# Loading the parameters first, four more warm-up matmuls, and the gate exponentials moved behind the last convolution tile

## The chip, the cores and the metric

The kernel runs on one core of one Trainium2 chip. The metric is the device time of one execution in microseconds (us). TensorE is called PE in the profile (its weight loads PEld), VectorE DVE, ScalarE ACT, GpSimd POOL, and SyncE, which here only issues DMAs, SP.

## What is computed

One decoder layer for a prompt of 512 tokens and a sample group of 8 x 8 tokens, 576 columns in all, model width 1024. The part that matters here is the first third:

```
u    = rms(x) * g_pre_mix;   proj = u @ w_in          # 1024 x 5656
z, xbc, dt_raw, q, k, v, ig, fg, og = split(proj)
xbc  = silu(causal_conv(xbc))                         # 12 tiles of 128 channels
dt   = softplus(dt_raw + dt_bias);  a = -exp(a_log)   # the gates
h'   = h * exp(cum[-1]) + sum_s exp(cum[-1]-cum_s) dt_s x_s B_s     # SSD state, per chunk
y    = (C B^T * exp(cum_t - cum_s) * dt) x + (C h) * exp(cum_t)
mLSTM heads from q, k, v, ig, fg with the same kind of chunk decays; then w_out
...                                                   # cross-attention, SwiGLU
```

## The kernel before, in words

Activations lie transposed: 128 features on the partitions, 576 tokens in the free dimension, eight such blocks `k`. A float32 product is made of three matmuls in a reduced float32 format: high part times high part, high times low, low times high. So each weight tile `raw` is split into `whi` (a cast, ACT, L186) and `wlo` (the rest, DVE L193, or ACT L190 and an accumulating DMA from POOL, L191), and the activations into `uh` and `ul`. The matmuls of a tile go in two halves of the tokens, 256 and 320 wide.

**The start.** PE first runs `NWARM` matmuls on a zeroed tile `wz` (L309, written to `ps_warm`, which nobody reads). Meanwhile SP and ACT issue the loads: for the first two weight tiles 256 columns at a time (`raws[0]`, `raws[1]`), the eight blocks of x (`xraw`), and `par`, a table of 128 x 150 numbers with all gains and biases. ACT makes `uh` from `xraw` and the gain in `par` (L333), DVE makes `ul` (L334). Then PE runs the first two weight tiles block by block (L350 to L352), the third (`w2`, L208 to L211), the sums of squares of x by a product with ones (`ps_ss`, L234), and the fourth tile (`w3`). ACT and DVE in the meantime split `w2`, sum the squares of x into `ssqx` (L270 to L275), and split `w3`.

**Convolution and gates.** `conv_tile(j, dst)` makes one of 12 convolution tiles: PE product, DVE eviction into `cb`, ACT and DVE taps into `ac`, and two Silu activations on ACT, 512 and 64 wide (L498, L500). Ahead of j = 4 the gate tile and the first q tile are put in. A chain of small operations on ACT and DVE turns the gates into running sums, which PE transposes (`ps_ct`) and spreads (`ps_en`). Seven exponentials on ACT, 4 to 64 columns wide, follow (L601 to L612): `decp` and `wend` (SSD decay and weight of each token in its chunk's end state), `scalem` and `wendm` (the same for mLSTM), `expnm`.

**The SSD part.** `ssd_prompt` takes four chunks in turn: PE transposes x (`ps_xt`), DVE scales it (`xdt`), POOL multiplies by `wend` (`xe`, L650), PE multiplies by B's tokens `btok` (`ps_h`, L652), POOL and DVE carry the state on (`hs`). PE mixes these with the products of q, k and v tiles (`ps_in`, `ps_v`), which need nothing of the gates.

Silu and Exp lie in different activation tables. The build step puts an ACT_TABLE_LOAD in front of an activation whose table is not the loaded one. The order of each engine's instructions in this part is set by a scheduler when the kernel is built; `tc.high_priority(offset=1000)` around the block from `ps_ct` on pulls it forward, and `tc.issue_after(x)` keeps what stands under it behind the instruction x.

Of the kernel before, what the change touches and what calls it, by code (L numbers as in the profile page):

```python
# [14 lines left out]
AF = mybir.ActivationFunctionType  # L15
# [5 lines left out]
T = 576  # L21
TP = 512
TS = 64
# [83 lines left out]

CUT = 512
CCUT = 128
NWARM = 17  # L110
NSS = 7
NWX = 3
TCOPT = dict(schedule_with_timeline_sim=True)
# [2 lines left out]
def build(nc, tc, ctx, I, O):  # L116
    V, A, G, S, TE = nc.vector, nc.scalar, nc.gpsimd, nc.sync, nc.tensor
# [21 lines left out]
    def MP(name="m"):  # L139
        return pa.tile([P, 512], F32, name=name, tag="a")  # L140
# [12 lines left out]
    par = cp.tile([P, NPAR], F32, name="par")  # L153

    def C32(k):
        a, b = _c32[k]
        return c32[:, a:b] if b <= NLONG else c32e[:, a - NLONG:b - NLONG]
# [5 lines left out]
    def PAR(k, j=None, w=1):  # L163
        a, b = _cols[k]
        return par[:, a:b] if j is None else par[:, a + j:a + j + w]
# [30 lines left out]
    def split(hi, lo, src, eng=None, cast=None):  # L196
        c = (cast or A.copy)(hi, src)  # L197
        (eng or V).tensor_tensor(lo, src, hi.bitcast(F32), op=ALU.subtract)  # L198
        return c
# [93 lines left out]
    wendm = ml.tile([P, 5, 4], F32, name="wendm")  # L293
    scalem = ml.tile([P, 4, 4], F32, name="scalem")
# [12 lines left out]
    psw = MP("ps_warm")  # L307
    for _ in range(NWARM):
        mm(psw[:, 0:256], wz[:, 0:128], wz, start=True, stop=True, skip_group_check=True)  # L309

    wl = [wp.tile([P, 1024], F32R, name="wlo", tag="wlo", bufs=3) for _ in range(2)]
    RT = {k: wp.tile([P, 3], F32, name=k + "_r", tag=k + "_r") for k in ("px0", "p30", "px1", "p31")}
# [2 lines left out]
    for k in range(KT):  # L315
        if k % 2 == 0:
            c = slice(128 * k, 128 * k + 256)
            S.dma_start(raws[0][:, c], I["win"][1][:, c])
        if k == 0:
            S.dma_start(par, I["par"])  # L320
        xd = (S if k else A).dma_start(xraw[:, k, :], I["xT"][:, k, :])
        if k % 2 == 0:
            xd = (S if k else A).dma_start(raws[1][:, c], I["win"][2][:, c])
        if k == 0:
            with tc.issue_after(xd.ins), tc.high_priority(offset=300):

                A.activation(sp.tile([P, 1], F32, name="one"), wz[:, 0:1], AF.Exp)

        if k == 0:
            V.tensor_copy(wi[0][0][:, c], raws[0][:, c])  # L330
        for t0, n in ([(0, T)] if k else HALVES):
            ts_ = slice(t0, t0 + n)
            uhk = A.activation(uh[:, k, ts_], xraw[:, k, ts_], AF.Copy, scale=PAR("g_pre", k))  # L333
            ulk = V.scalar_tensor_tensor(ul[:, k, ts_], xraw[:, k, ts_], PAR("g_pre", k), uh[:, k, ts_].bitcast(F32),  # L334
                                         op0=ALU.mult, op1=ALU.subtract)
        if k % 2 == 0:
            for i in range(2):
                with tc.issue_after(uhk.ins), tc.issue_after(ulk.ins):
                    split(wi[i][0][:, c], wi[i][1][:, c], raws[i][:, c], cast=None if k or i else lambda *_: None)
# [54 lines left out]
    def in_tile(i, evac, cut=CUT):  # L394

        if i < 5:
            for (t0, n), ps in zip(HALVES, ps0[i - 1]):
                if i == 4 and t0:
                    with tc.issue_after(rows[-1].ins):
                        gemm(ps, [(*w3, KT)], U, UL, t0, n, 2, KT)  # L400
                evac(t0, n, xs[:, 5 + i, t0:t0 + n] if i < 3 else ps)
        else:
            if i not in fetched:
                fetch(i, cut)
            w = fetched.pop(i)
            if i in behind:
                gemm2([(*w, KT)], U, UL, evac, "ps_in", [0])
            with tc.issue_after(behind[i].ins) if i in behind else ExitStack():
                gemm2([(*w, KT)], U, UL, evac, "ps_in", [1] if i in behind else [0, 1])
# [11 lines left out]
    wend = bcp.tile([P, 5, 16], F32, name="wend")  # L421
    decp = bcp.tile([P, 4, 16], F32, name="decp")
# [35 lines left out]
    cst = cv.tile([P, 12, NB, 3], F32, name="cst")  # L458
    S.dma_start(cst, I["convst"])

    late_rows, last_in = [], [5]

    def conv_tile(j, dst):

        cb = cv.tile([P, 604], F32, name="cb", tag="cb", bufs=2)
        sm = cb[:, CS:CB].rearrange("p (b t) -> p b t", t=11)

        def ev(t0, n, ps):
            V.tensor_tensor(cb[:, 3 + t0:259 + t0], ps[:, 0:256], rxb[:, t0:t0 + 256], op=ALU.mult)
            if t0:  # L470
                V.tensor_tensor(sm[:, :, 3:11], ps[:, 256:320].rearrange("p (b t) -> p b t", t=8),
                                rxb[:, TP:T].rearrange("p (b t) -> p b t", t=8), op=ALU.mult)

        in_tile(1 + j, ev, CUT if j == 4 else 0)
        with ExitStack() as after:
            if 4 <= j < 10:
                for i in range(2 + j, 4 + j):
                    if i > last_in[0]:
                        fetch(i, 0)
                        last_in[0] = i  # L480
                after.enter_context(tc.issue_after(accs[-1].ins))
            if late_rows:
                late_rows.pop()()
            G.memset(cb[:, 0:3], 0.0)
            G.tensor_copy(sm[:, :, 0:3], cst[:, j, :, :])

        def rows_out():
            G.tensor_copy(convo[:, j, 0:3], cb[:, CS - 3:CS])
            G.tensor_copy(convo[:, j, 3:27].rearrange("p (b t) -> p b t", t=3), sm[:, :, 8:11])

        late_rows.append(rows_out)
        e = V
        ac = cv.tile([P, 604], F32, name="ac", tag="ac", bufs=2)
        A.activation(ac[:, 0:600], cb[:, 0:600], AF.Identity, scale=PAR("convw", 4 * j), bias=PAR("convb", j))
        for k in range(1, 4):
            e.scalar_tensor_tensor(ac[:, 0:600], cb[:, k:600 + k], PAR("convw", 4 * j + k), ac[:, 0:600],
                                   op0=ALU.mult, op1=ALU.add)
        A.activation(dst[:, 0:TP], ac[:, 0:TP], AF.Silu)  # L498
        sa = ac[:, CS:CB].rearrange("p (b t) -> p b t", t=11)
        A.activation(dst[:, TP:T].rearrange("p (b t) -> p b t", t=8), sa[:, :, 0:8], AF.Silu)  # L500


    qk = SL(1, "qk")
# [82 lines left out]
    with tc.high_priority(offset=1000):  # L586
        psc = MP("ps_ct")
        for c in range(4):
            TE.transpose(psc[:, c * 104:c * 104 + 100], r1[:, c * P:(c + 1) * P], ident[0:100, 0:100])
            TE.transpose(psc[:, c * 104 + 100:c * 104 + 104], r2[:, c * P:(c + 1) * P], ident[0:4, 0:4])  # L590
        A.copy(CT[:, 0:4, :], psc[:, 0:416].rearrange("p (c k) -> p c k", c=4))
        psc = MP("ps_ct2")
        TE.transpose(psc[:TS, 0:100], r1[:, TP:T], ident[0:100, 0:100])
        TE.transpose(psc[:TS, 100:104], r2[:, TP:T], ident[0:4, 0:4])
        A.copy(CT[:TS, 4, :], psc[:TS, 0:104])
        pse = MP("ps_en")
        mm(pse[:, 0:416], C32("e127"), CT[:, 0:4, :].rearrange("p c k -> p (c k)"), start=True, stop=True)
        en = pse[:, 0:416].rearrange("p (c k) -> p c k", c=4)
        V.tensor_tensor(wend[:, 0:4, :], en[:, :, 0:16], CT[:, 0:4, 0:16], op=ALU.subtract)
        V.tensor_tensor(wendm[:, 0:4, :], en[:, :, 96:100], CT[:, 0:4, 64:68], op=ALU.add)  # L600
        A.activation(decp, en[:, :, 0:16], AF.Exp)  # L601
        A.activation(scalem, en[:, :, 96:100], AF.Exp)
        pse = MP("ps_en2")
        mm(pse[:TS, 0:104], C32("esamp")[:TS, :], CT[:TS, 4, :], start=True, stop=True)
        V.tensor_tensor(wend[:TS, 4, :], pse[:TS, 0:16], CT[:TS, 4, 0:16], op=ALU.subtract)
        V.tensor_tensor(wendm[:TS, 4, :], pse[:TS, 96:100], CT[:TS, 4, 64:68], op=ALU.add)
        A.activation(wend[:, 0:4, :], wend[:, 0:4, :], AF.Exp)
        A.activation(wendm[:, 0:4, :], wendm[:, 0:4, :], AF.Exp)
        A.activation(wend[:TS, 4, :], wend[:TS, 4, :], AF.Exp)
        wd = A.activation(wendm[:TS, 4, :], wendm[:TS, 4, :], AF.Exp)  # L610
        with tc.issue_after(wd.ins):
            A.activation(expnm, CT[:, 0:4, 100:104], AF.Exp, scale=-1.0)  # L612
        V.tensor_scalar(ncum, CT[:, 0:4, 0:16], -1.0, None, op0=ALU.mult)
# [126 lines left out]
    for g in range(2):  # L740
        for hb in range(2):
            dst = cpad[:, g, 4 * hb:4 * hb + 4, :].rearrange("p b t -> p (b t)")
# [5 lines left out]
    for g in range(2):  # L748
# [13 lines left out]
        for h in range(8):  # L762
            k, j = h % 2, (8 * g + h) // 2
# [164 lines left out]
    for h in range(4):  # L928
        q, k = qk[:, h, :], qk[:, 4 + h, :]
# [1488 lines left out]
```

## Time and profile before

| | |
|---|---|
| runs | 1078.0, 1080.8, 1081.1 us, median 1080.8 |
| profiled execution | 1079.13 us, its span 1077.4 us |
| busy share of the span | PE 99%, PEld 94%, DVE 70%, ACT 56%, POOL 21% |
| chain that ended last | PE 93%, DVE 3%, ACT 1%, DMA 1% |
| HBM | 159.75 MB read, 20.65 MB written |

The busy time of PE is modelled and includes the way through the array, so whether PE moves at its full pace is better read from the distance between the starts of two matmuls. In a row of the timeline the first number is the start, the second the duration, and the bracket holds the idle time in front with what ended it.

### The profile page before, as it was taken

The page shows a single profiled execution, that of the slowest core. Times are in us where ns is not written, and L with a number is a line of the kernel's source. Part 1 is how long each engine was busy: PE and PEld are TensorE (multiplying, and loading weights), DVE is VectorE, ACT ScalarE, POOL GpSimd, SP SyncE. Part 2 cuts the span into 40 slices and gives each one's busy share as a digit, 9 for nine tenths or more (in the row PEclk, how much of TensorE's full clock was granted, in tenths as well). Part 3 has the DMA queues.
Part 4 walks back from the last instruction along what each step waited for, and adds up shares of the span by engine and source line. Part 5 has one row for each costly group of instructions (what it writes and reads, how often), then busy time and mean ns, then how long its engine had stood idle before and what let it go on. Part 6 is the DMA issues. An engine that isn't in the chain of part 4 may idle for free.

```text
span 1077.4 us, 20699 instructions
## 1 busy us (share of the span) xinstructions
PE 1067.5 (99%) x8120; PEld 1015.1 (94%) x8120; DVE 752.0 (70%) x1509; ACT 607.8 (56%) x1094; POOL 231.5 (21%) x305
## 2 busy tenths in 40 slices
PE   9999999999999999999999999999999999999997
PEld 8999887778999999999999889999999999999997
DVE  6798775658877775559755555766467887787556
ACT  7778532345654555656555445645566566656653
POOL 0453643313213111000154301100011111111000
PEclk9999999999999999999999999999999999999998
DMA  6787544426655449743468775644476697588532
GB/s 208 164 171 133 159 127 177 147 73 183 191 153 145 111 120 329 254 169 109 147 206 286 268 257 176 241 131 93 136 181 140 155 201 167 116 190 184 130 132 89
DMA packets 58822, 181.76 MB, mean 169 GB/s; under 512 B 6588, under 2 KB 11836, under 8 KB 58212
## 3 DMA queue, kind: packets, MB, share of 16 engines
q1 hardware_dynamic: 42740, 138.06, 39.1%
q0 software_dynamic: 15408, 41.43, 20.0%
q8 instruction: 64, 1.05, 0.4%
q10 hardware_dynamic: 576, 0.95, 0.3%
q14 instruction: 34, 0.28, 0.1%
HBM read 159.75 MB, written 20.65 MB: 167 GB/s over the span
## 4 chain that ended last, share of the span: by engine, by line
PE 93%; DVE 3%; ACT 1%; DMA 1%; issue 1%; POOL 0%; DVEq 0%; SPq 0%; ACTq 0%
PE ps_in L208 6%; PE ps_in L211 6%; PE ps_in L209 6%; PE ps_v L854 5%; PE ps_o L211 3%; PE ps_g L1910 3%; PE ps_g L1909 3%; PE ps_o L209 3%; PE ps_g L1911 3%; PE ps_o L208 3%; PE ps_u L1910 3%; PE ps_u L1911 3%; PE ps_u L1909 3%; PE ps_dn L1909 2%; PE ps_dn L1910 2%; PE ps_dn L1911 2%
## 5 line engine op out<-in xcount | busy, mean ns | idle before, releaser
L211 PE MATMUL ps_in<-uh,wlo 128*128 128x320 f32 (+1 forms) x544 | 161.6, 298 | 0.0
L208 PE MATMUL ps_in<-uh,whi 128*128 128x320 f32 (+1 forms) x544 | 161.6, 297 | 0.0
L209 PE MATMUL ps_in<-ul,whi 128*128 128x320 f32 (+1 forms) x544 | 160.9, 296 | 0.0
L186 ACT CAST whi<-raw 128x1024 fp32r<-128x1024 f32 (+1 forms) x104 | 105.4, 1014 | 96.3 <-PE ps_in L209 30.2
L193 DVE TENSOR_TENSOR wlo<-raw,whi 128x1024 fp32r<-128x1024 f32 (+2 forms) x97 | 94.8, 979 | 61.8 <-ACT whi L186 57.3
L211 PEld LDWEIGHTS ps_in<-uh,wlo 128*128 128x128 f32 x544 | 102.2, 188 | 2.0 <-issue 1.3
L208 PEld LDWEIGHTS ps_in<-uh,whi 128*128 128x128 f32 x544 | 102.3, 188 | 1.5 <-issue 0.8
L209 PEld LDWEIGHTS ps_in<-ul,whi 128*128 128x128 f32 x544 | 102.3, 188 | 0.4
L191 POOL DMA_DIRECT2D wlo<-win x31 | 27.2, 876 | 76.0 <-ACT wlo L190 64.7
L1909 PE MATMUL ps_g<-b,whi 128*128 128x288 f32 x144 | 42.4, 295 | 0.0
L1910 PE MATMUL ps_g<-b,whi 128*128 128x288 f32 x144 | 42.4, 295 | 0.0
L1910 PE MATMUL ps_u<-b,whi 128*128 128x288 f32 x144 | 42.2, 294 | 0.0
L1909 PE MATMUL ps_u<-b,whi 128*128 128x288 f32 x144 | 42.2, 294 | 0.0
L1882 ACT CAST whi<-rawx 128x1024 fp32r<-128x1024 f32 (+1 forms) x26 | 25.7, 987 | 27.7 <-PE ps_dn L1910 13.7
L198 DVE TENSOR_TENSOR wlo<-sw,whi 128x1024 fp32r<-128x1024 f32 (+1 forms) x26 | 29.6, 1140 | 15.5 <-ACT whi L197 15.4
L208 PE MATMUL ps_xo<-qh,whi 128*128 128x288 f32 x128 | 38.4, 302 | 0.1
L211 PE MATMUL ps_o<-mixm_h,wlo 128*128 128x256 f32 (+1 forms) x128 | 37.7, 295 | 0.0
L209 PE MATMUL ps_xo<-ql,whi 128*128 128x288 f32 x128 | 37.7, 296 | 0.0
L209 PE MATMUL ps_o<-mixm_l,whi 128*128 128x256 f32 (+1 forms) x128 | 37.5, 293 | 0.0
L211 PE MATMUL ps_xq<-u2h,wlo 128*128 128x320 f32 (+1 forms) x128 | 37.5, 294 | 0.0
L209 PE MATMUL ps_xq<-u2l,whi 128*128 128x320 f32 (+1 forms) x128 | 37.4, 294 | 0.0
L211 PE MATMUL ps_o<-mixs_h,wlo 128*128 128x320 f32 (+1 forms) x128 | 37.4, 292 | 0.0
(770 smaller groups left out, 3848.6 us busy)
## 6 DMA issues: line engine op xcount, KB each, us to landing
raw<-win SPq DMA_DIRECT2D x35, 512.0 KB, 4.1
raw<-wout SPq DMA_DIRECT2D x17, 512.0 KB, 4.0
raw<-wxq SPq DMA_DIRECT2D x13, 512.0 KB, 4.0
raw<-wgate SPq DMA_DIRECT2D x13, 512.0 KB, 3.6
raw<-wup SPq DMA_DIRECT2D x13, 512.0 KB, 5.0
wlo<-win POOLq DMA_DIRECT2D x24, 256.0 KB, 5.1
kva<-vc SPq DMA_DIRECT2D x11, 512.0 KB, 6.5
raw<-wv SPq DMA_DIRECT2D x10, 512.0 KB, 4.1
```

Of the source, the lines that this page charges most:

```text
L186: casts.append(A.copy(hi[:, :n], raw[:, :n]))
L191: accs.append(G.dma_start(lo[:, a:b], src[:, a:b], accum_op=ALU.add))
L193: e.tensor_tensor(lo[:, a:b], raw[:, a:b], hi[:, a:b].bitcast(F32), op=ALU.subtract)
L198: (eng or V).tensor_tensor(lo, src, hi.bitcast(F32), op=ALU.subtract)
L208: mm(ps, wh, ah, start=i == 0, stop=False)
L209: mm(ps, wh, al, start=False, stop=False)
L211: m = mm(ps, tiles[order[c]][1], xh(order[c], t0, n), start=False, stop=c == len(tiles) - 1)
L854: mm(ps, a, b, skip_group_check=True, **kw)
L1882: A.copy(s.h3[:, s.all], s.r2[:, s.all])
L1909: mm(ps, wh, b[0][k], start=start and k == 0, stop=False, skip_group_check=True)
L1910: mm(ps, wh, b[1][k], start=False, stop=False, skip_group_check=True)
L1911: m = mm(ps, wl, b[0][k], start=False, stop=k == nk - 1, skip_group_check=True)
```

## The change

`NWARM` goes from 17 to 21. The load of `par` is issued right behind the warm-up matmuls in program order, ahead of the first piece of weights, and no longer between weights and x. The second Silu of every convolution tile is kept in a list; `decp` is issued behind the last one in that list, and `scalem`, `wend`, `wendm` behind `decp`.

```diff
-NWARM = 17
+NWARM = 21
...
     for _ in range(NWARM):
         mm(psw[:, 0:256], wz[:, 0:128], wz, start=True, stop=True, skip_group_check=True)
+    S.dma_start(par, I["par"])
...
             S.dma_start(raws[0][:, c], I["win"][1][:, c])
-        if k == 0:
-            S.dma_start(par, I["par"])
         xd = (S if k else A).dma_start(xraw[:, k, :], I["xT"][:, k, :])
...
-        A.activation(dst[:, TP:T].rearrange("p (b t) -> p b t", t=8), sa[:, :, 0:8], AF.Silu)
+        silus.append(A.activation(dst[:, TP:T].rearrange("p (b t) -> p b t", t=8), sa[:, :, 0:8], AF.Silu))
...
-        A.activation(decp, en[:, :, 0:16], AF.Exp)
-        A.activation(scalem, en[:, :, 96:100], AF.Exp)
+        with tc.issue_after(silus[-1].ins):
+            dx = A.activation(decp, en[:, :, 0:16], AF.Exp)
+        with tc.issue_after(dx.ins):
+            A.activation(scalem, en[:, :, 96:100], AF.Exp)
...
-        A.activation(wend[:, 0:4, :], wend[:, 0:4, :], AF.Exp)
-        A.activation(wendm[:, 0:4, :], wendm[:, 0:4, :], AF.Exp)
-        A.activation(wend[:TS, 4, :], wend[:TS, 4, :], AF.Exp)
-        wd = A.activation(wendm[:TS, 4, :], wendm[:TS, 4, :], AF.Exp)
+        with tc.issue_after(dx.ins):
+            A.activation(wend[:, 0:4, :], wend[:, 0:4, :], AF.Exp)
+            A.activation(wendm[:, 0:4, :], wendm[:, 0:4, :], AF.Exp)
+            A.activation(wend[:TS, 4, :], wend[:TS, 4, :], AF.Exp)
+            wd = A.activation(wendm[:TS, 4, :], wendm[:TS, 4, :], AF.Exp)
```

The scheduler's order changes with it. On SP, the first DMAs of the program, before (`raw` are weights, `xraw` is x):

```order
L318 DMA raw<-win 128x256
L320 DMA par<-par 128x150
L321 DMA xraw<-xT 128x576
L318 DMA raw<-win 128x256
L321 DMA xraw<-xT 128x576
```

and in the changed kernel:

```order
L310 DMA par<-par 128x150
L319 DMA raw<-win 128x256
L320 DMA xraw<-xT 128x576
L319 DMA raw<-win 128x256
L320 DMA xraw<-xT 128x576
```

Only `par` and the first piece of weights change places; the DMAs behind them keep their order up to the SSD part.

On ACT, around the exponentials, from a late convolution tile on, before:

```order
L500 ACTIVATE xs<-ac 128x64
L607 ACT_TABLE_LOAD
L607 ACTIVATE wend<-wend 128x64
L601 ACTIVATE decp<-ps_en 128x64
L602 ACTIVATE scalem<-ps_en 128x16
L608 ACTIVATE wendm<-wendm 128x16
L609 ACTIVATE wend<-wend 64x16
L610 ACTIVATE wendm<-wendm 64x4
L612 ACTIVATE expnm<-CT 128x16
L498 ACT_TABLE_LOAD
L498 ACTIVATE xs<-ac 128x512
```

and in the changed kernel, from the last convolution tile on:

```order
L499 ACTIVATE xs<-ac 128x64
L601 ACT_TABLE_LOAD
L601 ACTIVATE decp<-ps_en 128x64
L603 ACTIVATE scalem<-ps_en 128x16
L609 ACTIVATE wend<-wend 128x64
L610 ACTIVATE wendm<-wendm 128x16
L611 ACTIVATE wend<-wend 64x16
L612 ACTIVATE wendm<-wendm 64x4
L614 ACTIVATE expnm<-CT 128x16
L634 COPY btok<-ps_bt 128x512
```

The exponentials move behind the Silu activations of the last three tiles and now stand directly ahead of `btok`. The table load that led back to Silu goes, and so does a later one that led to Exp again (L754 before).

On PE, the rows around the first state product of the SSD part (`c_78` is the identity used for transposes), before:

```order
L209 MATMUL ps_in<-ul,whi 128x256
L652 MATMUL ps_h<-xe,btok 128x512
L644 MATMUL ps_xt<-c_78,xs 128x128 x4
L729 MATMUL ps_xts<-c_78,xs 64x128 x8
L211 MATMUL ps_in<-uh,wlo 128x256
```

and in the changed kernel:

```order
L208 MATMUL ps_in<-uh,whi 128x256
L654 MATMUL ps_h<-xe,btok 128x512
L646 MATMUL ps_xt<-c_78,xs 128x128 x4
L731 MATMUL ps_xts<-c_78,xs 64x128 x8
L209 MATMUL ps_in<-ul,whi 128x256
```

The group is the same, but it stands further back: between the products `ps_cb` of the same chunks and the first `ps_h` there are 68 weight-tile matmuls before and 97 now.

More of the change, by code (lines that the diff above doesn't have):

```diff
@@ L459, in build @@
     S.dma_start(cst, I["convst"])
-    late_rows, last_in = [], [5]
+    late_rows, last_in, silus = [], [5], []
     def conv_tile(j, dst):
```

## The prediction

> **What bounds the kernel now.** I read the page's busy shares and chain first, then what PE waited for, then the timeline of the two places that the change touches.
>
> ```profile
> PE 1067.5 (99%) x8120; PEld 1015.1 (94%) x8120; DVE 752.0 (70%) x1509; ACT 607.8 (56%) x1094; POOL 231.5 (21%) x305
> ...
> PE 93%; DVE 3%; ACT 1%; DMA 1%; issue 1%; POOL 0%; DVEq 0%; SPq 0%; ACTq 0%
> ```
>
> PE is the bound: 93% of the chain. All that PE itself waited for in the whole execution is three entries:
>
> ```profile
> PE ps_warm L309 <- DVE wz L306: 1.1, 1, 1.1
> PE ps_in L350 <- ACT uh L333: 1.0, 1, 1.0
> PE ps_ct L589 <- ACT r L567: 0.3, 1, 0.3
> ```
>
> So there is no stall of PE near the gate exponentials that their move could remove. What can be won lies at the start: the idle 1.0 us, and whatever runs there below full pace. The timeline of the start:
>
> ```profile
> 0.74 0.42 ACTq L321 DMA_DIRECT2D xraw<-xT  x1
> ...
> 1.06 3.81 PE L309 MATMUL ps_warm<-wz 128*128 128x256 bf16 x17 [1.06 <-DVE wz L306]
> ...
> 4.50 0.29 DVE L330 CAST whi<-raw 128x256 fp32r<-128x256 f32 x1 [3.50 <-DMA raw<-win]
> ...
> 5.35 0.96 ACT L333 ACTIVATE uh<-xraw,par 128x256 fp32r<-128x256 f32 x2 [2.19 <-DMA par<-par]
> ...
> 5.91 1.09 PE L350 MATMUL ps_in<-uh,whi 128*128 128x256 f32 x2 [1.04 <-ACT uh L333]
> ...
> 7.01 0.41 PE L350 MATMUL ps_in<-uh,whi 128*128 128x256 f32 x1
> ...
> 7.23 0.41 PE L351 MATMUL ps_in<-ul,whi 128*128 128x256 f32 x1
> ...
> 10.16 0.35 PE L351 MATMUL ps_in<-ul,whi 128*128 128x256 f32 x1
> ...
> 10.35 0.28 PE L352 MATMUL ps_in<-uh,wlo 128*128 128x256 f32 x1
> ...
> 10.47 0.31 PE L351 MATMUL ps_in<-ul,whi 128*128 128x320 f32 x1
> ```
>
> The warm-up ends at 4.87 (1.06 + 3.81), the first real matmul starts at 5.91: a hole of 1.04 us, whose end hangs on `uh`, and `uh` on the landing of `par`. The two matmuls at 7.01 and 7.23 are 256 wide and lie 0.22 us apart; those at 10.35 and 10.47 lie 0.12 apart. PE runs at half pace until about 10.25 and at full pace from there (the granted clock, third number from the end in this row of the stages, shows none of it):
>
> ```profile
> 5.00:10.00 5.00, 4.09 (x16) 3.92 (x17) 4.28 (x11) 4.03 (x9) 0.00 (x0) 1.00 1.02 345
> ```
>
> From 5.91 to 10.25 are 4.34 us at half pace, which cost 4.34 / 2 = 2.17 us.
>
> **The change part by part.**
>
> *`par` first.* It was issued second on SP; now the first piece of weights is. Then `uh` waits for x instead.
>
> ```profile
> xraw<-xT SPq DMA_DIRECT2D x7, 288.0 KB, 4.4
> ...
> par<-par SPq DMA_DIRECT2D x1, 75.0 KB, 4.1
> ```
>
> The first x block goes out on ACT's queue at 0.74; with the 4.4 us of its seven sisters it lands at 5.1 (an estimate), `par` at 0.74 + 4.1 = 4.8 at the latest. `uh` starts at 5.1 instead of 5.35 and the first real matmul 0.25 us earlier, near 5.66. From below, the moved weights could land 0.45 later than 4.50 (one issue slot), still ahead of `uh`'s end, so nothing is lost; from above, x might land with the weights' 4.50, 0.85 earlier. I take 0.25, the row of the same transfer.
>
> *Four more warm-up matmuls.* Seventeen took 3.81 us, so the distance is about (3.81 - 0.41) / 16 = 0.212 us. Twenty-one end at 1.06 + 20 x 0.212 + 0.41 = 5.71: the hole is closed, and if x should land early, they stand in the way by less than 0.3 us. What matters is the pace. A busy stretch of 3.81 us (1.06 to 4.87) did not bring the full pace; the next one, after the hole, brought it after 4.34 us. One stretch without a hole from 1.06 would bring it at 1.06 + 4.34 = 5.4, and nothing of the 2.17 us is left; in the worst case it still comes at 10.25, and only the 0.25 remain. So the start is worth 0.25 to 2.4 us; I take the upper end, since the hole is the only thing that sets the two stretches apart.
>
> The Trainium skill ("TensorE: Matmul & The Clock Gate", Part 1) says that the array is clocked at half rate until a free-running window of about 3.4 us has been busy throughout, so that the moment varies from run to run. By that rule the clock would open between 4.5 and 7.9 us after the change, and the start would be worth at least 0.25 + 2.17 - (7.9 - 5.66) / 2 = 1.3 us; the hole agrees with the rule, its length of window no row here shows.
>
> *What stops the gain.* The third and fourth weight tile hang on a chain that PE has no part in:
>
> ```profile
> 16.25 1.05 ACT L186 CAST whi<-raw 128x1024 fp32r<-128x1024 f32 x1 [1.19 <-DMA raw<-win]
> ...
> 24.48 2.02 ACT L186 CAST whi<-raw 128x1024 fp32r<-128x1024 f32 x2
> ```
>
> ```profile
> 17.33 1.23 DVE L193 TENSOR_TENSOR wlo<-raw,whi 128x1024 fp32r<-128x1024 f32 x1 [1.24 <-ACT whi L186]
> 18.49 5.93 DVE L275 TENSOR_TENSOR ssqx<-ssqx,sq 128x576 f32<-128x576 f32 x7
> 25.59 1.23 DVE L193 TENSOR_TENSOR wlo<-raw,whi 128x1024 fp32r<-128x1024 f32 x1 [1.16 <-ACT whi L186]
> ```
>
> ```profile
> 28.62 0.28 PE L211 MATMUL ps_in<-uh,wlo 128*128 128x256 f32 x1
> ```
>
> The weights `w2` land, are cast at 16.25, split at 17.33, then come seven sums of squares to 24.4, and only then `w3`: its `wlo` is ready at 25.59 + 1.23 = 26.82, and PE first reads it at 28.62. The loads in front of this keep their places, so 26.82 stays; PE can be at most 28.62 - 26.82 = 1.8 us earlier here. Of the 2.4 us this lets 1.8 through; the rest turns into a short wait of PE for `w3` or for the sums.
>
> *Does the 1.8 us last?* Behind it comes the gate chain, in which DVE is full:
>
> ```profile
> 60.00:80.00 20.00, 20.00 (x157) 20.00 (x157) 19.57 (x35) 13.00 (x21) 9.78 (x19) 1.00 0.78 167
> ```
>
> ```profile
> 39.55 0.43 ACT L448 COPY xg<-ps_in 40x320 f32<-40x320 f32 x1 [0.43 <-PE ps_in L445]
> ```
>
> DVE cannot catch up, but it doesn't have to: the chain begins at the gate tile, where ACT waited for PE, so it starts earlier by what PE has won.
>
> *The exponentials.*
>
> ```profile
> 91.45 1.28 ACT L607 ACT_TABLE_LOAD   x1
> 92.74 0.26 ACT L607 ACTIVATE wend<-wend 128x64 f32<-128x64 f32 x1
> ...
> 93.59 1.28 ACT L498 ACT_TABLE_LOAD   x1
> ...
> 105.45 0.63 ACT L498 ACTIVATE xs<-ac 128x512 f32<-128x512 f32 x1 [2.15 <-DVE ac L496]
> ...
> 106.14 0.57 ACT L632 COPY btok<-ps_bt 128x512 f32<-128x512 f32 x1
> ...
> 120.77 1.28 ACT L754 ACT_TABLE_LOAD   x1
> ```
>
> Of the three loads one is left: ACT gets 2 x 1.28 = 2.56 us back. It is worth nothing by itself, for ACT is not what PE waits for, and at 105.45 ACT idled for 2.15 us. The price is lateness: the seven exponentials, done at 93.59 before, now begin at 106.14 (or earlier by what PE has won) and take 1.28 + 0.85 (92.74 to 93.59) = 2.13 us, to 108.3 at the latest; `btok`, `cbs` and the weight cast queued behind them on ACT are up to 2.1 us later. Who waits for that:
>
> ```profile
> 98.99 0.60 PE L630 MATMUL ps_bt<-c,bc 128*128 128x128 f32 x4
> ...
> 109.25 1.02 PE L652 MATMUL ps_h<-xe,btok 128*128 128x512 f32 x2
> ```
>
> ```profile
> 106.44 1.04 POOL L650 TENSOR_TENSOR xe<-xdt,wend 128x512 f32<-128x512 f32 x1 [0.71 <-DVE xdt L646]
> ```
>
> `xe` can run from 108.3 to 109.3. In the new order `ps_h` has 29 weight-tile matmuls more ahead of it, at 0.12 us about 3.5 us, so PE reaches it at 109.25 + 3.5 - 1.8 = 111.0: 1.7 us of room. I count nothing, because weight tiles cover the wait; without that cover each microsecond past 111.0 is one of PE. PE's own work is the same, but for the four matmuls that fill the hole.
>
> **Sum.** 1079.1 (the profiled execution, 1.7 below the median shown) - 1.8 = 1077.3 us.
>
> **The rivals.**
>
> *The clock opens no earlier.* For it: the change does not touch what PE must wait for between 5.7 and 7, so that the new stretch is not quite without holes. Against it: those holes were there in the stretch that did open. Only 0.25 is left: 1078.9.
>
> *The limit of 1.8 doesn't hold.* If the loads behind `par` land earlier too, the chain from 16.25 on moves along and all of 2.4 is kept: 1076.7. Against it: nothing in the queue behind the first two rows changes.
>
> *Slower: the SSD part starves PE.* Room that was 12.8 us (93.59 to 106.44) shrinks to 1.7. The first chunk may fit and a later one not, since ACT has a block of long casts among them:
>
> ```profile
> 115.03 1.04 ACT L713 CAST stb<-xes 32x1024 fp32r<-32x1024 f32 x1 [6.22 <-POOL xes L736]
> ...
> 118.63 1.05 ACT L715 CAST stb<-xes 32x1024 fp32r<-32x1024 f32 x1
> ```
>
> From 115.03 to 119.68 they hold ACT for 4.65 us. If this block once falls between an `xdt` and its `ps_h`, PE loses about 4.65, in all 4.65 - 1.8 = 2.9 slower: 1082.0; twice, 1086.6. It decides from the point where `wend` comes after 110.0 (111.0 less the 1.04 of `xe`). Against it: the order was laid out with the late exponentials in it, and the order of before left PE without a wait.
>
> **How the numbers follow.** About 0.3% (3.2 us of 1080.8) is what a measurement of this kernel can tell from no change; the border of faster is 1077.6, and the forecast lies just beyond it. Chances: the forecast 0.62, no earlier clock 0.14, no limit 0.10, starving 0.12, something else 0.02. Of the forecast's 0.62, whose own range is 1076.7 to 1078.5, I put 0.38 beyond the border. Faster: 0.38 + 0.10 = 0.48. Slower: 0.10 of the starving case and the 0.02. Same: the rest, 0.40. The range goes from 1076.7 less 1.1, by which the lowest run shown (1078.0) lies under the profiled execution (1075.6), to 1078.9 plus 1.7, the median's distance from the profiled execution (1080.6).
>
> **What would show each step.** Right: the first real matmul near 5.7, two 256-wide matmuls 0.12 apart before 8; a short wait of PE near 24 to 27; `ps_bt` about 1.8 us earlier than 98.99; two table loads fewer, and no wait of PE at `ps_h`. Wrong: half pace until 10; `ps_bt` not earlier than 98.99 by more than 0.5; or entries of PE waiting for POOL `xe` or ACT `btok`.

## The result, and the profile after

The changed kernel takes 1084.9 us (median of 6 runs, 1084.1 to 1086.3) beside 1079.3 us for the kernel before on the same chip (6 runs). The ratio is 1.0054 (95% interval 1.0040 to 1.0067): it is slower by 5.6 us, where a gain of 1.8 us was forecast. The profiled execution took 1084.92 us, its span 1083.1.

What PE waited for in the changed kernel (who waited, for whom: us in total, times, longest), without the two entries at `ps_warm` and `ps_ct` that before has too:

```profile
PE ps_hu L798 <- DVE h L799: 1.8, 1, 1.8
PE ps_hu L798 <- ACT bm L793: 1.3, 1, 1.3
...
PE ps_yi L684 <- DVE lm L677: 0.5, 1, 0.5
PE ps_in L208 <- ACT la L448: 0.2, 1, 0.2
```

The 1.0 us in front of the first real matmul is gone, but three waits in the SSD part are new (`ps_hu` twice, `ps_yi`), 3.6 us together, where before had none. None of them is for `xe` or `btok`. The wait for `la` lies in the gate chain, at 38 us. `ps_hu` belongs to the states of the eight samples: POOL multiplies a state `h` by its decay (L795), ACT makes `bm` (L793), PE the outer product `ps_hu` (L798), DVE adds it to `h` (L799) and so frees its bank for a later `ps_hu`.

**The start** is as forecast. The timeline of the changed kernel (start, duration, engine, line; in the bracket the idle time ahead and what ended it):

```profile
1.06 4.66 PE L309 MATMUL ps_warm<-wz 128*128 128x256 bf16 x21 [1.06 <-DVE wz L306]
...
4.08 0.96 ACT L332 ACTIVATE uh<-xraw,par 128x256 fp32r<-128x256 f32 x2
...
5.37 0.83 PE L349 MATMUL ps_in<-uh,whi 128*128 128x256 f32 x2
...
8.09 0.28 PE L350 MATMUL ps_in<-ul,whi 128*128 128x256 f32 x1
8.21 0.28 PE L351 MATMUL ps_in<-uh,wlo 128*128 128x256 f32 x1
...
25.58 1.23 DVE L193 TENSOR_TENSOR wlo<-raw,whi 128x1024 fp32r<-128x1024 f32 x1 [1.16 <-ACT whi L186]
...
26.52 0.31 PE L209 MATMUL ps_in<-ul,whi 128*128 128x320 f32 x1
26.86 0.39 PE L211 MATMUL ps_in<-uh,wlo 128*128 128x256 f32 x1
...
97.66 0.60 PE L632 MATMUL ps_bt<-c,bc 128*128 128x128 f32 x4
...
109.69 1.38 POOL L652 TENSOR_TENSOR xe<-xdt,wend 128x512 f32<-128x512 f32 x1
...
112.03 1.02 PE L654 MATMUL ps_h<-xe,btok 128*128 128x512 f32 x2
```

At 8.09 two 256-wide matmuls already lie 0.12 us apart. The limit holds to the digit: `wlo` of `w3` is ready at 25.58 + 1.23 = 26.81, as before, and PE reads it at 26.86 instead of 28.62, 1.76 us earlier and 0.34 behind the matmul in front of it (320 columns wide, which otherwise lie 0.15 apart): 0.2 us lost to `w3`, too little to stand in the list of waits. `ps_bt` comes 1.33 us earlier than 98.99. And the first `xe` is done at 109.69 + 1.38 = 111.07, 0.96 us before PE comes to `ps_h`: the weight tiles do cover the late exponentials.

**Where it is lost.** First POOL and DVE of the changed kernel near 150 to 164 us, then PE behind them:

```profile
148.62 9.41 POOL L795 TENSOR_TENSOR h<-h,vt 128x1024 f32<-128x1024 f32 x4 [2.46 <-issue]
...
153.48 0.49 DVE L505 SCALAR_TENSOR_TENSOR qk<-ps_in,rxb 128x320 f32<-128x320 f32 x1 [3.94 <-PE ps_in L211]
...
154.49 4.62 DVE L193 TENSOR_TENSOR wlo<-raw,whi 128x1024 fp32r<-128x1024 f32 x2
...
161.08 2.14 DVE L674 SCALAR_TENSOR_TENSOR lm<-ps_l,ncum,c 128x128 f32<-128x128 f32 x8
...
163.75 0.67 DVE L799 TENSOR_TENSOR h<-h,ps_hu 128x512 f32<-128x512 f32 x1
```

```profile
162.41 0.31 PE L211 MATMUL ps_in<-uh,wlo 128*128 128x320 f32 x1
164.48 0.50 PE L798 MATMUL ps_hu<-stb,bm 96*128 96x512 f32 x1 [1.75 <-DVE h L799]
165.48 1.09 PE L684 MATMUL ps_yi<-lm,xdt 128*64 128x128 f32 x16 [0.50 <-DVE lm L677]
...
168.30 0.63 PE L856 MATMUL ps_v<-whi,ul 128*128 128x512 f32 x1
168.72 0.63 PE L856 MATMUL ps_v<-wlo,uh 128*128 128x512 f32 x1
...
170.41 0.40 PE L856 MATMUL ps_v<-whi,uh 128*128 128x512 f32 x1
170.65 0.39 PE L856 MATMUL ps_v<-whi,ul 128*128 128x512 f32 x1
```

and DVE at the same place in the kernel before:

```profile
150.40 2.35 DVE L193 TENSOR_TENSOR wlo<-raw,whi 128x1024 fp32r<-128x1024 f32 x1
...
154.61 1.21 DVE L193 TENSOR_TENSOR wlo<-raw,whi 128x1024 fp32r<-128x1024 f32 x1
```

In before two splits of 1024 columns stood apart with four short operations between them, and only one ran beside POOL's multiplies. In the changed kernel DVE idles 3.94 us first, then has both in a row beside POOL's last two multiplies. The first takes 1.74 us, the second 2.96, where one alone takes 1.21. The last multiply and the second split:

```profile
155.09 2.93 POOL L795 TENSOR_TENSOR h<-h,vt 128x1024 f32<-128x1024 f32 x1
156.15 2.96 DVE L193 TENSOR_TENSOR wlo<-raw,whi 128x1024 fp32r<-128x1024 f32 x1
```

Everything behind them is late: the `h` that frees the bank ends at 164.4, and PE stands still for 1.75 and 0.50 us. Behind that the 512-wide `ps_v` matmuls lie 0.42 us apart from 168.30 to 168.72, and 0.24 from 170.41 on: the full pace is lost for some 3.5 us. The stage shows it (PE busy, PEld, DVE, ACT, POOL, then the granted clock, DMA, GB/s); from 200 to 220 us the clock is at 1.00 again:

```profile
160.00:180.00 20.00, 17.74 (x107) 13.11 (x106) 14.23 (x33) 6.01 (x9) 3.30 (x4) 0.91 0.60 185
```

The third wait lies near 212 us. ACT of the changed kernel:

```profile
206.60 1.05 ACT L186 CAST whi<-raw 128x1024 fp32r<-128x1024 f32 x1 [3.45 <-DMA raw<-wv]
...
210.48 1.05 ACT L186 CAST whi<-raw 128x1024 fp32r<-128x1024 f32 x1 [2.24 <-DMA raw<-wv]
211.55 0.58 ACT L879 COPY vts<-ps_v 64x512 f32<-64x512 f32 x1
212.04 0.51 ACT L793 ACTIVATE bm<-sta,c 96x256 fp32r<-96x256 f32 x1
```

`bm` stands behind two casts whose weights land late, and PE waits 1.3 us for it. In before the last `bm` stood ahead of both casts (200.00, the casts at 202.28 and 204.48).

So the theory to test: **T**, the start gains and the late exponentials lose, not by being late but because the scheduler lays out the whole SSD part differently around them. The rivals: **R1**, the loss is their lateness itself; **R2**, the earlier start makes transfers and vector work collide later.

### The profile page after: what moved, and what is told of

Its sections match the earlier page's. It is cut to its first block, busy times and chain, and to the rows that moved or that the text cites. A ratio compares the mean times of both kernels' runs of the same rounds, so it can differ in the third digit from the quotient of the medians.

```text
span 1083.1 us, 20698 instructions
## 1 busy us (share of the span) xinstructions
PE 1070.7 (99%) x8124; PEld 1016.0 (94%) x8124; DVE 751.8 (69%) x1509; ACT 605.1 (56%) x1092; POOL 235.1 (22%) x305
## 4 chain that ended last, share of the span: by engine, by line
PE 88%; DVE 4%; DMA 3%; ACT 2%; issue 1%; POOL 0%; SPq 0%; DVEq 0%; ACTq 0%
PE ps_in L208 5%; PE ps_in L209 5%; PE ps_in L211 5%; PE ps_v L856 4%; PE ps_o L211 3%; PE ps_g L1912 3%; PE ps_g L1911 3%; PE ps_o L209 3%; PE ps_g L1913 3%; PE ps_o L208 3%; PE ps_u L1912 3%; PE ps_u L1913 3%; PE ps_u L1911 3%; PE ps_dn L1911 2%; PE ps_dn L1912 2%; PE ps_dn L1913 2%
```

## The experiments

Differences are medians against the kernel before in the same set of runs.

**1 and 2: each half alone.** First the start, on the kernel before; the SSD part keeps its order.

```diff
-NWARM = 17
+NWARM = 21
...
+    S.dma_start(par, I["par"])
...
-        if k == 0:
-            S.dma_start(par, I["par"])
```

> Part done alone: the parameters' load first and the warm-up of 21; the exponentials stay where the kernel before has them, so the SSD part's order is that of before. Theory T (the start gains, the other order of the SSD part loses): the lead at the first weight tiles is kept to the end, 1077.5 us (1.2 to 2.1 us under before). Rival R2 (the earlier start is what collides later with the transfers and the vector work): 1083 us or more, with waits of PE in the SSD part although its order is that of before.

Measured: 1077.8 us, 1.3 under before (ratio 0.9992, 0.9983 to 1.0000, so the gain is only just told from none), with 0.3 us of waits of PE in the whole SSD part. The second is the changed kernel with this half undone:

```diff
-NWARM = 21
+NWARM = 17
...
-    S.dma_start(par, I["par"])
...
+        if k == 0:
+            S.dma_start(par, I["par"])
```

> Part done alone: the gates' exponentials behind the last convolution tile's second activation; warm-up of 17 and the parameters' load as before, so the SSD part's order is that of the changed kernel. Theory T: 1086.5 us (some 7 us over before, without the start's gain), with PE's waits at ps_hu and ps_yi near 163 to 167 us and the granted clock below 1.00 in the stretch behind them. Rival R2: 1079 to 1080 us, no such waits.

Measured: 1085.8 us, 6.7 over before (1.0061, 1.0048 to 1.0074). The same three waits, and the same dip of the clock:

```profile
PE ps_hu L799 <- DVE h L800: 1.7, 1, 1.7
PE ps_hu L799 <- ACT bm L794: 1.5, 1, 1.5
...
PE ps_yi L685 <- DVE lm L678: 0.5, 1, 0.5
```

```profile
160.00:180.00 20.00, 17.75 (x110) 13.29 (x108) 14.39 (x32) 6.51 (x10) 3.75 (x4) 0.91 0.62 194
```

-1.3 and +6.7 make the +5.6 of the whole within 0.2. R2 has fallen: the start does no harm, and the waits are there without it.

**3: the two splits apart.** In the changed kernel the first two value weight units are held behind the first `added` (the `h` sum). One is set free:

```diff
-            with tc.issue_after(added[0].ins) if g == 0 and u < 2 else ExitStack():
+            with tc.issue_after(added[0].ins) if g == 0 and u == 1 else ExitStack():
```

> The changed kernel with one dependence less: unit 0 of the value weights may be split by DVE before the added step it was pinned behind, so DVE's two 1024-wide splits no longer stand together beside POOL's multiplies of the state; the exponentials stay behind the last convolution tile. Theory T: PE's wait of 2.3 to 2.7 us near 163 us and the fall of the clock behind it (1.7 us) go, the second wait (1.3 us, near 212 us) may stay: 1080.5 us. Rival R1 (the exponentials' own lateness is the loss, in whatever order): 1084.9 us as the changed kernel.

Measured: 1080.6 us, 1.5 over before (1.0017, 1.0008 to 1.0026), so 4.1 of the loss are gone with the exponentials as late as ever. The two splits on DVE, and what is left of PE's waits and of the dip:

```profile
141.18 1.21 DVE L193 TENSOR_TENSOR wlo<-raw,whi 128x1024 fp32r<-128x1024 f32 x1
...
154.80 1.73 DVE L193 TENSOR_TENSOR wlo<-raw,whi 128x1024 fp32r<-128x1024 f32 x1
```

```profile
PE ps_hu L798 <- ACT bm L793: 1.0, 1, 1.0
```

```profile
160.00:180.00 20.00, 20.00 (x132) 15.49 (x131) 14.23 (x30) 6.54 (x10) 6.00 (x5) 1.00 0.58 181
```

One split has gone into DVE's gap at 141, alone and so at 1.21 us; the other runs beside POOL at 1.73. R1 in its pure form has fallen.

**6: fill the standstill.** Does the clock fall because PE stands still? Sixteen matmuls that nobody reads go where PE stood still:

```diff
-            ps = (alloc or GP)(name)[:, :n]
+            bank = (alloc or GP)(name)
+            ps = bank[:, :n]
             m = gemm(ps, units, xh, xl, t0, n, order=order)
+            for _ in range(fill if i else 0):     # fill: 16 for the last q/k tile, else 0
+                mm(bank[:, 320:512], units[0][0][:, 0:P], xh(0, t0, 192), start=True, stop=True, ...)
```

> The changed kernel with 16 matmuls of 192 columns added behind the last query and key tile, into columns of its bank that nobody reads, so that PE works for some 1.5 to 1.9 us of the 2.7 us in which it stands idle near 163 us; nothing else computes on them. Theory (the clock falls because PE stands idle, and the slow ps_v matmuls behind it are slow for the clock): PE's idle time there falls under 1.3 us, the granted clock of 160 to 180 us is 1.00, the ps_v matmuls are 0.23 us apart, and the whole is 1.7 us shorter, 1083.2 us. Rival (the ps_v matmuls are slow for another reason, such as the transfers and vector work of that stretch): they stay 0.43 us apart and the whole stays at 1084.9 us or above.

Measured: 1081.5 us, 1.9 over before (1.0024, 1.0014 to 1.0035), 3.7 better than the changed kernel although PE has more to do. The two splits still stand together on DVE (4.61 us). PE's timeline and the stage:

```profile
161.66 1.93 PE L222 MATMUL ps_in<-uh,whi 128*128 128x192 f32 x16
...
164.16 1.09 PE L688 MATMUL ps_yi<-lm,xdt 128*64 128x128 f32 x16
...
167.28 0.39 PE L860 MATMUL ps_v<-wlo,uh 128*128 128x512 f32 x1
167.50 0.39 PE L860 MATMUL ps_v<-whi,uh 128*128 128x512 f32 x1
```

```profile
160.00:170.00 10.00, 9.90 (x70) 8.45 (x70) 7.80 (x18) 3.21 (x5) 1.41 (x2) 1.00 0.69 249
```

`ps_v` is 0.22 apart (167.28 to 167.50), the clock stays at 1.00. In the three traces with the standstill (the changed kernel, the second and the fifth experiment) the clock of 160 to 180 us is 0.83 to 0.91, in all others it is 1.00. From the start of `ps_yi` to that of the seventh `ps_v` are 167.50 - 164.16 = 3.34 us here and 170.41 - 165.48 = 4.93 in the changed kernel: the dip cost 1.59 us. That is the part I had expected; the other 2.1 us of the 3.7 are not the filler's own doing: the rows behind it were laid out a little differently, and the wait at `bm` is gone as well. So of this run only the stretch counts as shown.

**5: one row of PE.** In the changed kernel a `ps_hu` splits a group of four `ps_hs` matmuls one to three. The groups cost PE 5.3 us of busy time instead of 4.3 (the group of instructions in before, then in the changed kernel; behind the count busy us and mean ns):

```profile
L785 PE MATMUL ps_hs<-h,cpad 128*32 128x512 f32 x32 | 4.3, 605 | 0.0
```

```profile
L787 PE MATMUL ps_hs<-h,cpad 128*32 128x512 f32 x32 | 5.3, 605 | 0.0
```

```diff
-                mm(psh[q:q + 32, :], ...)
+                with tc.issue_after(hu[0].ins) if b == 1 else ExitStack():   # hu: the ps_hu matmuls
+                    mm(psh[q:q + 32, :], ...)
```

> The changed kernel with one row of PE's order moved: the first ps_hu matmul stands behind the first four ps_hs matmuls of the next group in the changed kernel's order only by splitting that group one to three; here it stands ahead of the group, as in the kernel before, and nothing else moves on any engine. Theory (the split group costs a ps_hs group's time once more): PE's time at ps_hs falls from 4.95 to 3.98 us and the whole from 1084.9 to 1083.9 us. Rival (the split costs nothing, the 0.97 us only lie elsewhere): 1084.9 us.

Measured: 1085.9 us, 6.3 over before (1.0063, 1.0050 to 1.0076): no gain, a miss.

```profile
L788 PE MATMUL ps_hs<-h,cpad 128*32 128x512 f32 x32 | 4.3, 605 | 0.0
```

```profile
164.48 0.60 PE L799 MATMUL ps_hu<-stb,bm 96*128 96x512 f32 x1 [2.30 <-DVE h L800]
165.48 1.97 PE L684 MATMUL ps_yi<-lm,xdt 128*64 128x128 f32 x16 [0.40 <-DVE lm L677]
...
171.65 0.39 PE L857 MATMUL ps_v<-whi,uh 128*128 128x512 f32 x1
```

The microsecond was saved, and PE waited it away: `ps_hu` starts at 164.48 and `ps_yi` at 165.48 as in the changed kernel, since DVE sets them. And the longer standstill (2.30 + 0.40 instead of 1.75 + 0.50, and another 0.5 some 5 us ahead of it) brought the dip earlier, with `ps_yi` itself at 1.97 instead of 1.09: from `ps_yi` to the seventh `ps_v` are 171.65 - 165.48 = 6.17 us, so it cost 2.83 instead of 1.59.

**9 and 10: the same rows where no wait for DVE follows.** The ninth is the third and the fifth together.

> The third experiment's kernel (unit 0 unpinned) and the fifth's row move together: one ps_hu matmul stands ahead of the group of four ps_hs matmuls that it split. In the fifth PE arrived earlier at a wait for DVE and lost there what it had gained; here PE does not wait for DVE. Theory (work taken from PE shortens the time where no wait of PE follows it): ps_hs 0.97 us shorter and the whole 1079.6 us, 1 us under the third experiment. Rival (a split group never costs anything on the path): 1080.6 us.

Measured: 1079.75 us, 0.2 over before (0.9998, 0.9989 to 1.0007); the third was 1.5 over. Here the row is worth 1.3 us where 1.0 was expected; the two intervals, of two sets of runs, just miss each other. The tenth adds one row on ACT:

```diff
-                A.copy(o, p2[TS:P])
+                with tc.issue_after(bms[7].ins):       # bms: the bm activations
+                    A.copy(o, p2[TS:P])
```

> As the ninth, and ACT's copy of the last value product stands behind the last bm in place of ahead of it. Theory (the second wait of PE, at ps_hu for bm near 210 us, is ACT's queue): the wait shrinks by that copy's 0.5 to 0.6 us, from 1.0 to about 0.5 us, and the whole is 1079.1 us. Rival (PE meets another wait at once): the wait at bm shrinks and the whole stays where the ninth is.

Measured: 1079.55 us, level with before (1.0001, 0.9991 to 1.0010). The wait for `bm`, ninth and tenth:

```profile
PE ps_hu L799 <- ACT bm L794: 1.2, 1, 1.2
```

```profile
PE ps_hu L799 <- ACT bm L794: 0.4, 1, 0.4
```

The wait shrinks by 0.8 us, so it is ACT's queue; the time by 0.2, which is within the uncertainty, so what this wait was worth is not settled.

**4, 11 and 12: the exponentials behind tile 10, 9 and 8.** Each is the changed kernel with another entry of the list, `silus[-2]` (fourth), `silus[-3]` (eleventh) or `silus[-4]` (twelfth):

```diff
-        with tc.issue_after(silus[-1].ins):
+        with tc.issue_after(silus[-2].ins):
```

> The changed kernel with the exponentials behind tile 10's activation in place of the last tile's, about 5 us earlier; the order of the SSD part differs from both kernels. Rival R1: the loss shrinks with the lateness, about 1082 us. Theory T: the time goes by the order that comes out and not by the lateness: anywhere from 1078 to 1086 us, and whatever is over 1077.5 us shows as waits of PE in the SSD part or a granted clock below 1.00 there.

> The changed kernel with the exponentials behind tile 9's activation, some 10 us earlier than behind the last tile's; the order of the SSD part differs from that of before. Rival R1 (lateness is the loss): between the start edits alone (1077.8 us) and the fourth experiment (1081.3 us), 1079.5 us. Theory T (the order is the loss, whatever the lateness): the first group of ps_hs is split two to two here as in the fourth, and the whole is near the fourth's 1081.3 us.

> The changed kernel with the exponentials behind tile 8's activation, where the order of the SSD part on every engine comes out as that of the kernel before. Theory T: the start's gain is kept, 1077.8 us, the same as the start edits alone, and no wait of PE near 163 or 212 us. Rival R1: 1078.5 us or more, since the exponentials still run later than in before.

| behind | `decp` starts | order of the SSD part | median | against before |
|---|---|---|---|---|
| last tile (changed kernel) | 105.4 | its own | 1084.9 | +5.6 |
| tile 10 | 99.7 | its own | 1081.3 | +2.2 |
| tile 9 | 94.3 | its own | 1080.9 | +1.3 |
| tile 8 | 91.5 | as before | 1077.9 | -1.7 |
| last tile, ninth experiment | 104.5 | its own, experiments 3 and 5 in it | 1079.75 | +0.2 |

Tile 9 is only 2.8 us later than tile 8 and 3.0 us dearer; the ninth experiment has the exponentials 10 us later than tile 9 and is 1.1 us faster. In the first four rows the time grows with the lateness, as R1 has it, but out of proportion: 2.8 us more cost 3.0, the next 5.4 only 0.9. The last row does not fit R1 at all. The time goes by the order, not by the lateness. Tile 8 hardly delays them (`decp` started at 92.91 before), so it is no test of lateness, as my expectation took it to be. It is the version that beats both kernels: 0.9982 (0.9973 to 0.9991) of before, and as fast as the start alone.

In the trace of the fourth experiment PE waits 1.2 us for `bm` and 0.3 us for `xe`, the latter at 131 us, 30 us behind the exponentials. The clock dips there too, but at another place, ahead of the SSD part, where it is at 1.00 in the traces of all other versions:

```profile
80.00:100.00 20.00, 20.00 (x135) 18.87 (x134) 16.48 (x35) 14.58 (x27) 6.52 (x17) 0.91 0.62 130
```

**7 and 8: which of the two start edits.** The diff of the first experiment in two: the seventh has its first two lines, the eighth the rest.

> The kernel before with only the warm-up of 21 in place of 17; the parameters' load and the exponentials as before, order of the SSD part as before. Theory (the start's gain is the clock, which the longer warm-up opens sooner): nearly all of the 1.3 us that both start edits gave, 1077.9 us. Rival (the gain comes from the parameters' earlier landing): 1079.1 us.

> The kernel before with only the parameters' load moved ahead of the first weights; warm-up of 17 and the exponentials as before, order of the SSD part as before. Theory (the gain is the clock, and the earlier first matmuls close part of the hole behind a warm-up of 17): between 1077.9 and 1079.1 us, 1078.6 us. Rival (the gain comes from the earlier landing alone): 1077.9 us, and the longer warm-up alone gives nothing.

Measured: 21 warm-up matmuls alone 1078.4 us, 1.2 under before (0.9994, 0.9985 to 1.0004); `par` first alone 1077.9 us, 1.7 under (0.9991, 0.9981 to 1.0002). Each alone gives what both give; the difference between them is less than these intervals can tell, and neither alone is clear of no change. Nor is the clock before always as late as in its profiled execution. From 6 to 8 us PE started 8 matmuls there, and 13 in the second experiment, whose start is the same; in the runs with one or both edits they were 13 to 17:

```profile
6.00:8.00 2.00, 2.00 (x8) 1.83 (x9) 2.00 (x6) 2.00 (x5) 0.00 (x0) 1.00 1.08 354
```

```profile
6.00:8.00 2.00, 1.93 (x13) 1.73 (x13) 2.00 (x6) 2.00 (x6) 0.00 (x0) 1.00 1.06 366
```

## Why the prediction was wrong

- **`par` first: right, small.** x landed earlier than the 5.1 that I had worked out, `uh` started at 4.08, and the longer warm-up then stood in the way of the first matmul (5.37, forecast 5.66).
- **The clock: right in this trace, but not for the reason given.** Full pace came at about 6.6 us (256-wide matmuls at 6.00, 6.21 and 6.42, 0.21 apart; 320-wide ones at 6.60 and 6.75, only 0.15 apart): before 8, as forecast, but later than the 5.4 I had worked out. That only the hole set the two stretches apart was wrong. The second experiment has the same 17 warm-up matmuls and a hole of 1.10 us. Its warm-up took 3.57 us instead of 3.81, its last two matmuls 0.12 us apart, so full pace came ahead of the hole, and behind the hole it was still there (matmuls at 6.80 and 6.92). I had taken the one profiled start of before, half pace until 10.25, as its usual one. The two edits are worth 1.3 us in the first experiment (0 to 1.8 by its interval) and 1.7 in the twelfth (1.0 to 2.9). That the 1.8 lies close to this is in part luck.
- **The limit of 1.8: right**, 1.76 measured, with a short wait of 0.2 us for `w3`. What else was won is lost there.
- **Lasts through the gate chain: right**, 1.33 us are left at `ps_bt`, and the start alone keeps 1.3 to the end, within the uncertainty above.
- **The exponentials: the step that failed.** "I count nothing, because weight tiles cover the wait." The cover held: nothing waits for `wend`. What I left out is that moving them re-laid the order of some hundreds of rows, as far as 230 us. I priced the moved instructions and not the new order. It cost 6.7 us: 4.1 for the two splits standing together (a standstill of 1.75 + 0.50 us and a clock dip of 1.59, in all 3.84, by the traces), 1.3 for the split `ps_hs` group, 0.2, not certain, for `bm`. From the tenth experiment to the start alone 1.3 us are left (level with before, against 1.3 under), whose cause stays open; 0.4 of it may be the wait that is left.
- **The rival "slower: the SSD part starves PE"** had the side and, at 1082.0 to 1086.6, the size, but neither the place nor the mechanism: DVE at 160 us, not ACT's casts of `stb`. My argument against it, that the order was laid out with the late exponentials in it and before's left PE without a wait, was no evidence: the order that the scheduler laid out with them did make PE wait on the chip. Whether it reckons with a split that takes up to 2.96 us beside POOL was not tried.

## What to carry to other kernels

Where a scheduler sets the order, a pin on a few small instructions is a change to everything behind them: compare the order of each engine over the whole part, and look for long operations that now stand together in front of something PE waits for. A pin that leaves the order alone (here tile 8) keeps the other gains. And shortening PE's work ahead of a wait buys nothing; if the wait then is long enough to lose the clock, it costs.

## What the runs showed of the hardware

**The clock can fall after less than 3 us of standstill.** A standstill of 1.75 and 0.50 us with one matmul between brought a dip that cost 1.59 us, 2.30 and 0.40 one that cost 2.83; single waits of 1.0 to 1.5 us for `bm` brought none (the clock of 205 to 220 us is at 1.00 in the second and the fifth experiment). The Trainium skill ("TensorE: Matmul & The Clock Gate", "Why this matters for your kernels") asks for no gaps of over about 3 us. Here the two gaps together were shorter than that, so for this kernel the measurement decides: gaps under 3 us are not safe.

No safe length takes its place. In the fourth experiment a wait of 0.33 us and 1.8 us of small transposes (`ps_ct`, 79.44 to 81.28) stand ahead of the dip: from 82.3 to 84.2 us the 320-wide matmuls lie 0.27 us apart instead of 0.15. The kernel before has the same transposes behind a wait of 0.34 us, at 81.33, and its clock stays at 1.00. What decides between the two no run here shows.

**A split on DVE and a multiply on POOL took turns.** Alone the split takes 1.21 us and POOL's multiply of 1024 columns 1.93. In the changed kernel the first split starts at 154.49, in the middle of POOL's third multiply (153.20 to 155.14), and ends at 156.23, 1.09 us behind that multiply's end. The fourth multiply then takes 2.93 us and ends at 158.02, and the second split ends at 159.11, again 1.09 behind it. The split of 2.35 us in before ends 1.07 us behind a multiply's end (151.68), the one of 1.73 in the third experiment 1.09 (155.44). By these rows each waits for the other's running instruction to end, and what a split costs depends on how much of the multiply is left when the split comes. The Trainium skill ("GPSIMD Engine Reference", "1. Specifications") says that POOL shares its interfaces to SBUF with VectorE and contends with its instructions of two SBUF inputs. The split is one, and the trace agrees.
